# Another fixed order for layer 0's projection tiles in a two-layer hybrid trunk

## The chip, the cores and the metric

One core of a Trainium2 chip runs the whole program. The time is the device time of one execution, in microseconds (us). Of the kernel before there are three timed runs, given as their median, lowest and highest, and one profiled execution with a time of its own. Lower is better.

## The reference

The input is a residual stream of 1024 tokens by 1024 features in float32 and a conditioning vector `c`. Two layers follow, and a final RMSNorm. Each layer normalises, scales and shifts its input by values that come from `c`, runs a mixer and adds the gated result. Layer 0 is the one that the change concerns:

```python
def even_mixer(h, w_in, ...):
    p = h @ w_in
    p_a, u, v, z = jnp.split(p, [SHIFT_W, SHIFT_W + B_WIDTH, SHIFT_W + 2 * B_WIDTH], axis=-1)
    y_a = rwkv7_time_mix(p_a, ...)             # r, k, v, and two low-rank inputs
    y_b = chunked_spatial_gate(u, v, ...)      # the gated layer (gMLP)
    y = jnp.concatenate([y_a, y_b], axis=-1) * jax.nn.silu(z)
    return y @ w_out

def step(S, inp):                              # inside rwkv7_time_mix, one token after the other
    r_t, w_t, k_t, v_t, kk_t, a_t = inp
    sa = jnp.einsum('bhvk,bhk->bhv', S, -kk_t)
    S = S * w_t[:, :, None, :] + sa[..., None] * (kk_t * a_t)[:, :, None, :] + v_t[..., None] * k_t[:, :, None, :]
    y_t = jnp.einsum('bhvk,bhk->bhv', S, r_t)
    return S, y_t
```

So `h @ w_in` has columns of five kinds: r, k and v of the recurrence (8 heads of 64), u and v of the gated layer (8 groups of 64), z for the gate over both, and a low-rank part. Layer 1 is a windowed attention whose code the change leaves alone.

## The kernel before, in words

**Tiles.** A projection tile is 128 columns of `w_in`, which is two heads or two groups. It is computed in two halves of 512 tokens. One half is 24 matmuls of 128x512 into one PSUM buffer (`gproj`, line 264: eight blocks of features, each times three products of high and low parts, since float32 is split in two). The tile's weights come by two DMAs of 256 KB on SP's queue (`wfetch`, line 232) and are split by ScalarE and GpSimd (`wsplit`, line 240), one tile ahead. When a half is complete, its evacuation empties the PSUM buffer: `krv_evac` (line 316) for r, k and v, one ScalarE and one VectorE pass into one of six `krv` buffers; `z_evac`, `u_evac`, `v_evac` and `zg_evac` for the rest. There are two PSUM buffers for projections.

Tile numbers, for the pair of heads j = 0 to 3: r is j, k is 4+j, v is 8+j; u of the gated layer is 13+j, its v is 17+j; z for the recurrence's half is 21+j and z for the gated half is 25+j. Tile 12 and the first pair's k, r and v (4, 0, 8) are computed ahead of the list, in `FIRST`.

**Units.** A unit is one pair of heads over half of the tokens; there are eight, numbered 2j and 2j+1. Each goes through four steps: `front` (line 559) takes k, r and v from the `krv` buffers and makes the operands; `solve` (line 664) builds the chunk matrices (the matmuls into `A` and `pM`) and inverts them, by a loop of 30 short VectorE instructions (lines 714 and 715) between `LN` (line 702) and `ZT` (line 719); `prep` (line 776) makes the transition matrices, and its last VectorE instruction is the one on line 804; `scan` (line 807) runs the chain of states. `front` of unit n starts when its three `krv` halves are there and `solve` of unit n-1 has passed its matrices. `solve` of unit n cannot start before `front` of unit n has given it its operands.

**What sets the order.** TensorE's order is written by hand. `drive` (line 1174) is a small planner that runs when the kernel is built: it keeps a model clock, and at each turn lets the thread of highest priority that is ready issue its next piece. `scan` has priority 0, `prep` and `solve` 1, `front` 2, the gated layer's `gm_tail` 4, the conditioning rows (`do_ada`) and the output weights (`wo0_thread`) 5, and `stream` (line 989), which issues the projection tiles, 6. A `yield` with a number tells the planner how long the piece's result takes, a `yield` with a function that the thread must wait for it. So the tiles fill the spaces that the units leave on TensorE, one matmul at a time, and on the chip TensorE runs what was written in that order, and stands still where an instruction's operands are late. The other engines are ordered by the compiler's scheduler, with the units' pieces given priority.

**Rooms.** After a half's matmuls, `stream` waits for the tile's room (lines 980 to 985): for r, k and v that fewer than six `krv` buffers are held (`held`). `front` gives the three halves of a unit back one at a time: k after `f` (line 583), r after `AR` (line 621), v after `bv` (line 660), and `bv` waits until the unit two before has been posted. For z there may be two `gz` waiting, for u two `uT`, and the gated layer's v shares three buffers with the conditioning rows.

**The list.** `ORDER` (line 987) is the fixed order of the 25 tiles behind `FIRST`. Written by name it is: z0, k1, r1, v1, gv0, u0, k2, r2, z1, v2, zg0, gv1, k3, r3, z2, v3, u1, zg1, z3, gv2, u2, zg2, gv3, u3, zg3 (gv for the gated layer's v, zg for its gate).

**After the list.** `out0_thread` (line 1118) starts layer 0's output projection when the list is done, the output weights are split and all but the last unit and the last gated half are posted. `wo0_thread` can split its last nine weight tiles only when the last `scan` has been issued, because they take the recurrence's memory.

Of the kernel before, what the change touches and what calls it, by code (L numbers as in the profile page):

```python
# [93 lines left out]
def tile_kernel(ctx, tc, x, cons, par, rows, ada, ada0, ew, wup, sgw, sgb, ewo, ow, owo, out, dbg=None):  # L94
# [889 lines left out]
        evac[13 + j], room[13 + j] = u_evac(j), lambda: short[0] < 2  # L984
        evac[25 + j], room[25 + j] = zg_evac(j), lambda: True

    ORDER = (21, 5, 1, 9, 17, 13, 6, 2, 22, 10, 25, 18, 7, 3, 23, 11, 14, 26, 24, 19, 15, 27, 20, 16, 28)

    def stream():
        todo = list(ORDER)  # L990
        for i in range(4):
            if i == 1:
                raws = wfetch(ew[todo[0]])
            pt = (yield from gproj(ws[i], 1)) if i else pt1
            FIRST[i][1](1, pt)
            if i == 1:
                w = wsplit(raws)
        while todo:
            n = todo.pop(0)
            raws = wfetch(ew[todo[0]]) if todo else None  # L1000
            pt = yield from gproj(w, 0)
            yield room[n]
            evac[n](0, pt)
            if todo:
                wn = wsplit(raws)
            pt = yield from gproj(w, 1)
            yield room[n]
            evac[n](1, pt)
            if todo:
                w = wn  # L1010
        done["h1"] = new_h()
# [470 lines left out]
```

## Time and profile before

| | us |
|---|---|
| median of 3 runs | 1106.13 |
| lowest, highest | 1104.96, 1108.74 |
| the profiled execution's own time | 1109.73 |
| its span, first to last instruction | 1107.6 |
| mean granted TensorE clock over the span | 0.983 |
| TensorE busy in the span | 1040.8 |
| VectorE busy in the span | 696.3 |
| ScalarE busy in the span | 524.3 |

In the profile a line gives start and duration of an instruction in us, its engine (PE is TensorE, DVE VectorE, ACT ScalarE, POOL GpSimd, SP the queue of most DMAs), its line in the kernel, and what it writes and reads. In brackets stands how long the engine had been idle and what released it. Adjoining instructions of one kind are merged, with their number behind an x. Matmuls are pipelined: one of 128x512 is shown as about 0.39 us long, but the next one starts 0.23 us behind it.

The projection tiles of layer 0 that the list orders run from 96 us to 615 us of the span.

### The profile page before, as it was taken

The page shows a single profiled execution, that of the slowest core. Times are in us where ns is not written, and L with a number is a line of the kernel's source. Part 1 is how long each engine was busy: PE and PEld are TensorE (multiplying, and loading weights), DVE is VectorE, ACT ScalarE, POOL GpSimd, SP SyncE. Part 2 cuts the span into 40 slices and gives each one's busy share as a digit, 9 for nine tenths or more (in the row PEclk, how much of TensorE's full clock was granted, in tenths as well). Part 3 has the DMA queues.
Part 4 walks back from the last instruction along what each step waited for, and adds up shares of the span by engine and source line. Part 5 has one row for each costly group of instructions (what it writes and reads, how often), then busy time and mean ns, then how long its engine had stood idle before and what let it go on. Part 6 is the DMA issues. An engine that isn't in the chain of part 4 may idle for free. (4 is left out here: it accounts for less than half of the span.)

```text
span 1107.6 us, 20700 instructions
## 1 busy us (share of the span) xinstructions
PE 1040.8 (94%) x7887; PEld 839.4 (76%) x7888; DVE 696.3 (63%) x1668; ACT 524.3 (47%) x1247; POOL 374.7 (34%) x483
## 2 busy tenths in 40 slices
PE   6989999999988898989999899999999999999997
PEld 3667778777776676766878777778888888878886
DVE  4455958586859485595642578864565654488754
ACT  4465555454454435445332233335565654487521
POOL 2333315141335122263423100134554544467201
PEclk9989999999999899999999899999999999999999
DMA  9501121212112121123122554421110111252121
GB/s 365 224 17 39 58 77 49 68 49 77 58 61 69 46 86 58 40 79 113 60 79 74 188 183 153 156 68 39 39 39 20 39 39 39 63 176 72 63 95 58
DMA packets 55131, 93.42 MB, mean 84 GB/s; under 512 B 5748, under 2 KB 15988, under 8 KB 55032
## 3 DMA queue, kind: packets, MB, share of 16 engines
q1 hardware_dynamic: 45176, 77.36, 21.3%
q10 hardware_dynamic: 9856, 14.75, 4.2%
q8 instruction: 62, 1.02, 0.4%
q14 instruction: 37, 0.30, 0.1%
HBM read 79.49 MB, written 12.59 MB: 83 GB/s over the span
## 5 line engine op out<-in xcount | busy, mean ns | idle before, releaser
L118 PE MATMUL pproj<-lo,whi 128*128 128x512 f32 x696 | 281.2, 404 | 0.0
L118 PE MATMUL pproj<-hi,whi 128*128 128x512 f32 x696 | 279.5, 402 | 0.7 <-ACT vt L1247 0.7
L118 PE MATMUL pproj<-hi,wlo 128*128 128x512 f32 x696 | 279.7, 402 | 0.0
L246 POOL TENSOR_TENSOR wlo<-wraw,whi 128x512 fp32r<-128x512 f32 x86 | 113.8, 1343 | 167.5 <-ACT whi L245 166.5
L118 PEld LDWEIGHTS pproj<-lo,whi 128*128 128x128 f32 x696 | 131.6, 189 | 24.9 <-issue 1.5
L118 PEld LDWEIGHTS pproj<-hi,whi 128*128 128x128 f32 x696 | 131.5, 189 | 24.5 <-ACT vt L1247 1.1
L118 PEld LDWEIGHTS pproj<-hi,wlo 128*128 128x128 f32 x696 | 131.3, 189 | 24.5 <-issue 1.2
L245 ACT ACTIVATE whi<-wraw 128x512 fp32r<-128x512 f32 x102 | 58.7, 622 | 65.9 <-PE htp L122 22.1
L118 PE MATMUL op<-wo,whi 128*128 128x512 f32 x256 | 82.2, 402 | 0.0
L1283 ACT ACTIVATE Sx<-Sx,nm 128x257 f32<-128x257 f32 (+1 forms) x128 | 62.3, 489 | 27.6 <-DVE nm L1279 25.5
L1279 DVE CUSTOM_DVE_ANT_0 Sx<-pS,bias,nsink 128x256 f32<-128x256 f32 (+1 forms) x128 | 53.4, 463 | 30.1 <-PE pS L118 28.6
L1287 POOL TENSOR_SCALAR Sx<-Sx,rc 128x256 f32<-128x256 f32 (+1 forms) x128 | 60.8, 492 | 25.4 <-DVE rc L1285 22.9
L1299 DVE TENSOR_TENSOR PL<-pT,PH 128x512 fp32r<-128x512 f32 (+1 forms) x64 | 41.6, 654 | 29.7 <-ACT PH L1298 29.2
L118 PEld LDWEIGHTS op<-wo,whi 128*128 128x128 f32 x256 | 49.0, 192 | 13.0 <-issue 2.1
L925 DVE SCALAR_TENSOR_TENSOR adacc<-araw,cond,adacc 128x512 f32<-128x512 f32 x56 | 44.0, 786 | 18.5 <-DMA araw<-ada 18.4
L118 PE MATMUL op<-hi,yh 128*128 128x512 f32 (+1 forms) x136 | 51.8, 381 | 0.4 <-ACT yh L1397 0.4
L118 PE MATMUL op<-hi,yl 128*128 128x512 f32 (+1 forms) x136 | 51.7, 380 | 0.4 <-DVE yl L1398 0.4
L118 PE MATMUL op<-wo,wlo 128*128 128x512 f32 x128 | 51.7, 404 | 0.0
L118 PE MATMUL op<-lo,yh 128*128 128x512 f32 (+1 forms) x136 | 51.5, 379 | 0.0
L213 POOL TENSOR_TENSOR st<-st,nhalf 128x1 f32<-128x1 f32 x16 | 9.6, 602 | 102.6 <-DVE st L212 91.0
L714 DVE TENSOR_TENSOR pr<-Lf,LT 128x2 f32<-128x2 f32 (+14 forms) x120 | 42.5, 354 | 2.7
L1298 ACT ACTIVATE PH<-pT 128x512 fp32r<-128x512 f32 (+1 forms) x64 | 35.7, 563 | 17.5 <-PE pT L1293 16.2
(317 smaller groups left out, 2166.5 us busy)
## 6 DMA issues: line engine op xcount, KB each, us to landing
araw<-ada SPq DMA_DIRECT2D x64, 256.0 KB, 2.8
wraw<-ew SPq DMA_DIRECT2D x50, 256.0 KB, 3.0
wraw<-ow SPq DMA_DIRECT2D x36, 256.0 KB, 3.0
adaraw<-ada SPq DMA_DIRECT2D x16, 512.0 KB, 9.0
x<-x SPq DMA_DIRECT2D x8, 512.0 KB, 8.7
woraw<-ewo SPq DMA_DIRECT2D x16, 256.0 KB, 2.9
xr<-x ACTq DMA_DIRECT2D x16, 256.0 KB, 3.5
wraw<-y0d SPq DMA_DIRECT2D x16, 256.0 KB, 3.1
```

The source lines that it names most:

```text
L118: last[0] = nc.tensor.matmul(out, lhsT=lhsT, rhs=rhs, **kw).ins
L213: G.tensor_tensor(out=st[:, 3:4], in0=st[:, 2:3], in1=nhalf[:, 0:1], op=ALU.pow)
L245: a = S.activation(hi[:, gs, :], raws[g], AF.Copy)
L246: b = E.tensor_tensor(out=lo[:, gs, :], in0=raws[g], in1=hi[:, gs, :].bitcast(F32), op=ALU.subtract)
L714: V.tensor_tensor(out=pr[:, 0:nc_, 0:i + 1], in0=Lf[:, i:i + 1, 0:i + 1].to_broadcast([P, nc_, i + 1]), in1=LTt[:, 0:nc_, 0:i + 1], op=ALU ...
L925: op = V.scalar_tensor_tensor(out=acc, in0=raw, scalar=cond[:, k:k + 1], in1=acc, op0=ALU.mult, op1=ALU.add)
L1279: V.tensor_tensor_reduce(out=Sx[:, e, off:2 * P], in0=pS3[:, e, 0:nk], in1=bias[e][:, off:], scale=1.0, scalar=nsink[:, hd:hd + 1], op0=AL ...
L1283: S.activation(pr[:, e, off:2 * P + 1], Sx[:, e, off:2 * P + 1], AF.Exp, bias=nm[:, e:e + 1], scale=-1.0, accum_out=sm[:, e:e + 1])
L1287: G.tensor_scalar(out=pr[:, e, off:2 * P], in0=pr[:, e, off:2 * P], scalar1=rc[:, e:e + 1], scalar2=0.5, op0=ALU.mult, op1=ALU.mult)
L1298: S.activation(PH[:, ks, :], pT2[:, ks, :], AF.Copy)
L1299: V.tensor_tensor(out=PL[:, ks, :], in0=pT2[:, ks, :], in1=PH[:, ks, :].bitcast(F32), op=ALU.subtract)
```

## The change

One line is changed, the list:

```diff
-    ORDER = (21, 5, 1, 9, 17, 13, 6, 2, 22, 10, 25, 18, 7, 3, 23, 11, 14, 26, 24, 19, 15, 27, 20, 16, 28)
+    ORDER = (21, 5, 1, 9, 17, 6, 2, 10, 22, 13, 25, 7, 3, 11, 23, 18, 14, 26, 24, 19, 15, 27, 20, 16, 28)
```

By name, the part that differs:

```
before  ... gv0, u0, k2, r2, z1, v2, zg0, gv1, k3, r3, z2, v3, u1, zg1 ...
after   ... gv0, k2, r2, v2, z1, u0, zg0, k3, r3, v3, z2, gv1, u1, zg1 ...
```

In the list k2 and r2 come one tile earlier, v2 two, u0 four later; k3 and r3 come one tile earlier, v3 two, gv1 four later. The tiles before gv0, zg0 in the middle, and everything from u1 on keep their places in the list. What is computed is the same. Because `drive` writes TensorE's order out anew from the list, where each matmul of the tiles falls between the units' pieces can change from there to the end of layer 0.

## Prediction

> **What bounds the kernel now.** I read the page first, then busy time by stretches, then the timeline of TensorE, VectorE and ScalarE around each unit of the recurrence. Columns of a stretch: the stretch and its length; busy us of PE, PEld, DVE, ACT and POOL (instructions); granted clock, DMA share, GB/s.
>
> ```profile
> PE 1040.8 (94%) x7887; PEld 839.4 (76%) x7888; DVE 696.3 (63%) x1668; ACT 524.3 (47%) x1247; POOL 374.7 (34%) x483
> ```
>
> ```profile
> 100.00:300.00 200.00, 187.86 (x1994) 149.03 (x1993) 143.96 (x348) 100.63 (x230) 58.15 (x49) 1.00 0.20 62
> 300.00:500.00 200.00, 177.55 (x1820) 139.76 (x1818) 137.42 (x309) 92.67 (x210) 66.80 (x51) 0.97 0.20 62
> ```
>
> TensorE is the bound, and in this stage it is filled by the tiles that the list orders. Its work is the same before and after, so only its idle time and its slow clock can be won. In 100 to 300 us it idles 12.1 us, in 300 to 500 us 22.4 us, with the clock down to 0.97. The difference, 10.3 us of idle time, and 0.03 x 200 = 6.0 us of clock are the most that a better order could win there.
>
> What the change aims at is the recurrence. VectorE's line 804 ends a unit's `prep`, its line 690 is the first product of the next unit's matrices. Units 1 to 2, 3 to 4 and 5 to 6:
>
> ```profile
> 209.84 0.69 DVE L804 TENSOR_TENSOR PA<-pn,dC 128x512 f32<-128x512 f32 x1
> 212.73 0.42 DVE L690 TENSOR_TENSOR BR<-A,rcon 128x256 f32<-128x256 f32 x1 [1.55 <-PE pM L118]
> 319.76 0.68 DVE L804 TENSOR_TENSOR PA<-pn,dC 128x512 f32<-128x512 f32 x1
> 326.26 0.42 DVE L690 TENSOR_TENSOR BR<-A,rcon 128x256 f32<-128x256 f32 x1 [1.25 <-PE pM L118]
> 445.71 0.69 DVE L804 TENSOR_TENSOR PA<-pn,dC 128x512 f32<-128x512 f32 x1
> 463.08 0.42 DVE L690 TENSOR_TENSOR BR<-A,rcon 128x256 f32<-128x256 f32 x1 [1.69 <-PE pM L118]
> ```
>
> The step takes 2.9 us, then 6.5, then 17.4. The excess, 3.6 and 14.5 us, are units 4 and 6 waiting for their `front`, and that waited for v2 and v3:
>
> ```profile
> 289.05 0.67 ACT L301 ACTIVATE krv<-pproj,der 128x512 f32<-128x512 f32 x1
> 394.31 1.07 DVE L702 STREAM_TRANSPOSE LN<-Dg 128x512 f32<-128x512 f32 x1
> 424.87 0.69 ACT L301 ACTIVATE krv<-pproj,der 128x512 f32<-128x512 f32 x1
> 430.80 0.68 DVE L583 TENSOR_TENSOR f<-krv,f 128x512 f32<-128x512 f32 x1
> ```
>
> `front` of unit 6 was free to start when unit 5 had its matrices (`LN`, 394.3 us), but v3's first half was evacuated at 424.9 us and `f` followed at 430.8.
>
> **When the moved tiles arrive.** No row shows the new order, so I take the stream's places as they are and put the new tiles into them. v2's first half takes the place of r2's, v3's first half that of r3's:
>
> ```profile
> 249.28 0.69 ACT L301 ACTIVATE krv<-pproj,der 128x512 f32<-128x512 f32 x1
> 273.91 1.04 DVE L702 STREAM_TRANSPOSE LN<-Dg 128x512 f32<-128x512 f32 x1
> 395.74 0.69 ACT L301 ACTIVATE krv<-pproj,der 128x512 f32<-128x512 f32 x1
> 594.06 0.28 DVE L821 SCALAR_TENSOR_TENSOR PA<-chain,dC,PA 128x64 f32<-128x64 f32 x1 [1.56 <-PE chain L118]
> ```
>
> So v2 comes near 249 instead of 289 us, v3 near 396 instead of 425. The first is 25 us ahead of unit 3's `LN` (273.9), the second 1.4 us behind unit 5's. Both waits should go: the last scan ends some 3.6 + 14.5 = 18 us sooner than at 594.3 us (the last of these rows).
>
> ```profile
> 440.00:460.00 20.00, 19.38 (x151) 15.41 (x151) 8.93 (x20) 8.54 (x17) 6.05 (x4) 1.00 0.12 41
> ```
>
> That is not 18 us of time. In the long wait, at 440 to 460 us, TensorE idled 0.6 us: it had tiles to run. With the wait gone those tiles are run elsewhere: more are left over behind the last scan, each half at its bare length, as two neighbouring halves show:
>
> ```profile
> 543.39 0.60 ACT L955 ACTIVATE uT<-pproj 128x512 f32<-128x512 f32 x1 [0.74 <-PE pproj L118]
> 548.86 0.60 ACT L955 ACTIVATE uT<-pproj 128x512 f32<-128x512 f32 x1 [4.87 <-PE pproj L118]
> ```
>
> A half costs 5.5 us wherever it stands; 24 matmuls moved are 24 matmuls. The same holds for what goes with a tile: its two DMAs on SP (256 KB, 3.0 us to landing), two splits on ScalarE and two on GpSimd are issued once per tile, a tile of two halves ahead, so at least 11 us of TensorE cover 3.0 us of fetch. I cost them at nothing; without that cover a tile would cost up to 3.0 us.
>
> ```profile
> wraw<-ew SPq DMA_DIRECT2D x50, 256.0 KB, 3.0
> ```
>
> **The sum: which stalls go.**
>
> ```profile
> 420.00:440.00 20.00, 16.09 (x251) 12.14 (x251) 11.30 (x16) 12.62 (x28) 6.81 (x5) 0.91 0.23 67
> 432.00:436.00 4.00, 4.00 (x43) 3.48 (x35) 2.82 (x4) 1.71 (x4) 1.21 (x2) 0.57 0.21 65
> ```
>
> ```profile
> 431.76 0.69 PE L118 MATMUL pM<-Zq,M 32*32 32x32 f32 x32 [1.80 <-ACT M L766]
> 310.29 1.94 PE L118 MATMUL uw<-PA,Z 128*128 128x128 f32 x15 [1.41 <-ACT Z L773]
> ```
>
> First, unit 6's late `front` runs into the end of unit 5's `solve`: the 1.80 us stall waits for a small copy on ScalarE behind that `front`'s activations. Stretch 420 to 440 idles 3.9 us where the rate of 100 to 300 us gives 20 x 12.1/200 = 1.2. Gain 2.7, at most 3.9 and at least nil, if the planner puts another stall there. Second, behind that stall the clock is halved for a piece: 0.09 x 20 = 1.8 us lost in the stretch. Gain 1.8. Third, unit 4's late `front` does the same at the end of unit 3's `solve`: gain 1.4 (bounds 0 and 1.4, since a weight split stood in ScalarE's way there too). Fourth, a cost: the two `front`s now run in a place that was empty; 440 to 460 idled 0.6 us instead of 1.2, and by the same rate I charge 0.6 for it. Fifth, the end of the stage:
>
> ```profile
> 614.06 1.19 DVE L1104 TENSOR_TENSOR wo<-woraw,wo 128x512 fp32r<-128x512 f32 x1
> 615.17 0.16 DVE L886 TENSOR_SCALAR gst<-gst 128x8 f32<-128x8 f32 x1
> 615.05 0.60 ACT L851 ACTIVATE ggz<-pproj 128x512 f32<-128x512 f32 x1 [1.09 <-PE pproj L118]
> 617.99 1.98 PE L118 MATMUL mix<-sgwt,vn 128*64 128x128 f32 x16 [3.26 <-DVE vn L890]
> ```
>
> TensorE stands 3.26 us for the last gated half, whose statistics (615.17) queue on VectorE behind a 1.19 us split of output weights. These splits wait for the last scan, so with the scan 18 us earlier they are over by then. Gain 1.2 of the 3.26; the rest, the gated half's own chain behind zg3, stays late.
>
> The tiles that move back, u0 and gv1, cost nothing in this sum: zg0 and zg1, which use what they leave, keep their places, and u0 and gv1 are still ahead of them, with u1 between gv1 and zg1 (two halves, 11 us). If that is too short for gv1's statistics, TensorE stands as at the last `mix`, up to 3.26 us.
>
> Sum: 2.7 + 1.8 + 1.4 - 0.6 + 1.2 = 6.5 us. The profiled execution would go from 1109.73 to 1103.2. It lies 3.6 us above the median of 1106.13; the same gain from the median gives 1099.6. Layer 1 keeps its code and its order, and I put no change there.
>
> A rule to weigh: the rows show the clock at 0.57 behind a stall of 1.80 us, but TensorE back at 1.00 for the whole of 440 to 460. The Trainium skill, "TensorE: Matmul & The Clock Gate", section "HAM oscillation — how this bites in real kernels", states that idle gaps above about 3.4 us are to be avoided. By that alone a 1.80 us stall halves nothing and the second term would be nil, a sum of 4.7; the trace disagrees, and I keep 1.8. The same page, "What's actually happening", has the activity window run freely, by which a like stall may or may not cost a piece.
>
> **The rivals.** *No change worth measuring.* The planner writes a new interleaving, and the stalls move. For it: 300 to 500 us has other stalls that have nothing to do with v2 and v3. The largest is unit 4's `ZT`, 3 us behind a loop that shares VectorE with zg0's evacuation and the gated layer's tail, and a slow clock after it:
>
> ```profile
> 361.57 0.65 PE L118 MATMUL pM<-ZT,Dg 16*32 16x32 f32 x32 [2.99 <-DVE ZT L719]
> 364.00:368.00 4.00, 4.00 (x75) 3.13 (x74) 1.31 (x4) 1.48 (x4) 0.00 (x0) 0.56 0.15 50
> ```
>
> Stretch 364 to 368 loses 0.44 x 4 = 1.8 us, with the stall 4.8. One new collision of that kind leaves 6.5 - 4.8 = 1.7 us of gain: 1104.4.
>
> *Slower.* VectorE becomes the late one in the loops of units 3 and 5. These had no `front` beside them; unit 2's loop had one. `LN` and `ZT` of unit 2, then `ZT` of units 3 and 5 (their `LN` stand above) with the matmul that takes it:
>
> ```profile
> 219.16 1.04 DVE L702 STREAM_TRANSPOSE LN<-Dg 128x512 f32<-128x512 f32 x1 [0.93 <-ACT Dg L696]
> 238.42 0.40 DVE L719 TENSOR_TENSOR ZT<-Tm,rcon 128x256 f32<-128x256 f32 x1
> 288.83 0.42 DVE L719 TENSOR_TENSOR ZT<-Tm,rcon 128x256 f32<-128x256 f32 x1
> 298.45 0.75 PE L118 MATMUL pM<-ZT,Dg 16*32 16x32 f32 x64
> 412.37 0.42 DVE L719 TENSOR_TENSOR ZT<-Tm,rcon 128x256 f32<-128x256 f32 x1
> 420.01 0.75 PE L118 MATMUL pM<-ZT,Dg 16*32 16x32 f32 x64
> ```
>
> With a `front` the stretch from `LN` to `ZT` takes 19.3 us in unit 2, without one 14.9 in unit 3: a `front` costs about 4.4. TensorE takes unit 3's `ZT` 9.2 us after it is ready and unit 5's 7.2, so 4.8 and 2.8 us would be left. It decides when the loop of unit 5 grows by over 7.2 us and that of unit 3 by over 9.2. If both do, two collisions of unit 4's kind cost 9.6, and with the clock halved twice as long, as the rows cannot exclude, 13.2: 3 to 7 us slower, 1109 to 1113. Against it: both have room left.
>
> *The change doesn't do what it says.* v2's second half needs a free `krv` buffer, given back by unit 3's `bv`:
>
> ```profile
> 253.86 0.69 DVE L660 TENSOR_TENSOR bv<-bon,krv 128x512 f32<-128x512 f32 x1
> 258.85 0.69 ACT L301 ACTIVATE krv<-pproj,der 128x512 f32<-128x512 f32 x1 [0.40 <-PE pproj L118]
> ```
>
> The buffer is free at 253.9 and the half's place ends at 258.9, 5.0 us of room. If the stream stops there, everything behind it on TensorE's list loses one half of filler, 5.5 us, and the gain shrinks to 1.0: 1105.1.
>
> **How the numbers follow.** About 0.3%, 3.3 us, is what a measurement of this kernel can tell from no change. The forecast has 0.50, no change 0.25, VectorE late 0.20, the stopped stream 0.05. Of the forecast 0.03 fall within 3.3 us; the no-change case gives 0.03 to faster and 0.02 to slower, VectorE late 0.03 to same, the stopped stream 0.02 to faster and 0.03 to slower. Faster 0.52, same 0.26, slower 0.22. The low end takes the whole excess idle time and the end term plus half of the clock's 6.0: 10.3 + 1.2 + 3.0 = 14.5, 1091.6. The high end is near that of VectorE late, 1112. The forecast's own range is 1091.6 to 1102.8, the upper end being a gain of 3.3 with the second and third term at nil.
>
> **What would show it.** Right: line 804 to 690 within 4 us at units 4 and 6; `f` of unit 6 near 400 us; the last scan near 576; 300 to 500 us idling under 18 us with a clock of 0.98 or more; the stall before the last `mix` near 2 us; zg3's last evacuation near 609 instead of 615.05. Wrong: a `ZT` stall at units 3 or 5, a stall of 2 us or more at a place that had none, or the scan early and zg3 not.

## The result, and the profile after

| | before | after |
|---|---|---|
| median, us | 1106.47 | 1098.41 |
| lowest, highest | 1104.96, 1108.74 (4 runs) | 1097.57, 1100.28 (4 runs) |
| the profiled execution: span, own time | 1107.6, 1109.73 | 1096.3, 1098.15 |
| mean granted clock in the profiled execution | 0.983 | 0.992 |

The change is faster: the ratio is 0.9928, with a 95% interval of 0.9906 to 0.9949, or 8.1 us. The prediction was 1099.6 us. The profiled executions differ by more, 11.3 us of span, because the one of before had a slower clock than its kernel usually has: over the 59 timed executions of the kernel before that this study has, the mean span is 1105.5 us and the clock 0.988, which is 1105.5 x 0.012 = 13.3 us lost to it; over the four of after 1096.8 us and 10.2 us lost. By this estimate, which counts every half-clock microsecond as half lost and sets executions on several chips side by side, some 3 of a mean gain of 8.7 us are clock and 5.5 are time in which TensorE works instead of standing.

The two stretches of the prediction, for after (columns as there):

```profile
100.00:300.00 200.00, 186.32 (x1994) 147.98 (x1994) 147.15 (x353) 104.86 (x239) 62.55 (x51) 1.00 0.20 62
300.00:500.00 200.00, 182.93 (x2088) 144.66 (x2088) 142.87 (x325) 96.15 (x222) 62.30 (x50) 0.97 0.21 65
```

From 300 to 500 us TensorE idles 17.1 us instead of 22.4, from 100 to 300 it idles 13.7 instead of 12.1. The clock of the stretch is the same to two decimals.

The handovers to units 4 and 6 in after, VectorE's timeline; then v2's and v3's first halves, unit 6's `f` and the last scan:

```profile
319.55 0.69 DVE L804 TENSOR_TENSOR PA<-pn,dC 128x512 f32<-128x512 f32 x1
323.12 0.42 DVE L690 TENSOR_TENSOR BR<-A,rcon 128x256 f32<-128x256 f32 x1 [2.23 <-PE pM L118]
440.06 0.69 DVE L804 TENSOR_TENSOR PA<-pn,dC 128x512 f32<-128x512 f32 x1
443.21 0.42 DVE L690 TENSOR_TENSOR BR<-A,rcon 128x256 f32<-128x256 f32 x1 [1.20 <-PE pM L118]
```

```profile
247.85 0.69 ACT L301 ACTIVATE krv<-pproj,der 128x512 f32<-128x512 f32 x1
391.20 0.69 ACT L301 ACTIVATE krv<-pproj,der 128x512 f32<-128x512 f32 x1
396.54 0.68 DVE L583 TENSOR_TENSOR f<-krv,f 128x512 f32<-128x512 f32 x1
570.99 0.28 DVE L821 SCALAR_TENSOR_TENSOR PA<-chain,dC,PA 128x64 f32<-128x64 f32 x1 [1.56 <-PE chain L118]
```

Both waits are gone: 3.6 us where there were 6.5, 3.2 where there were 17.4. The last scan is 23.1 us earlier. Of these 23 us, 2.1 were there before the first moved tile, as is shown next; of the other 21, 6 reach the last projection.

Where the 11.3 us of the two profiled executions lie is seen at two marks, the evacuation of the last gated half and the first score matmul of layer 1. The evacuation in after (that of before, at 615.05 us, stands in the prediction), then the score matmul in before and in after:

```profile
606.88 0.60 ACT L851 ACTIVATE ggz<-pproj 128x512 f32<-128x512 f32 x1 [2.40 <-PE pproj L118]
757.91 0.22 PE L118 MATMUL pS<-KH,Q 128*128 128x128 f32 x1
746.60 0.22 PE L118 MATMUL pS<-KH,Q 128*128 128x128 f32 x1
```

The first mark comes 615.05 - 606.88 = 8.2 us sooner, the second 11.3: the end of layer 0 gives another 3.1, and layer 1 gives nothing. Of the 8.2, 2.1 stand ahead of the first tile that changed place (gv0's last half is evacuated at 196.3 us in before and 194.2 in after), and there TensorE's order is the same; it is clock:

```profile
60.00:80.00 20.00, 17.43 (x72) 11.82 (x71) 10.99 (x14) 13.25 (x26) 5.76 (x6) 0.82 0.08 23
60.00:80.00 20.00, 16.63 (x73) 11.26 (x72) 12.28 (x16) 15.04 (x29) 7.62 (x9) 0.91 0.08 24
```

The first row is of before, the second of after: 0.09 x 20 = 1.8 us. So the 11.3 us are 2.1 of clock that have nothing to do with the change, 6.0 between gv0 and the last projection, and 3.1 behind it. In the 6.0, TensorE's idle time falls from 31.4 to 26.2 us and the clock loses 5 us instead of 7.

**The stalls that went.** The 1.80 us at unit 5's matrices, the 1.12 us at its `uw` behind it, the 1.41 us at unit 3's `uw` and 1.60 us at unit 6's `ZT` (501 us) are not there any more. Nor is a stall that the prediction did not see, at the first gated half behind zg1. Before, then after:

```profile
482.02 1.09 PE L118 MATMUL mix<-sgwt,vn 128*64 128x128 f32 x16 [3.26 <-DVE bst L897]
481.60 1.09 PE L118 MATMUL mix<-sgwt,vn 128*64 128x128 f32 x16
```

Behind it the clock of before is 0.79 from 482 to 490 us, 1.7 us lost; in after it is 1.00 there.

At the end of the stage, in after:

```profile
593.50 0.70 DVE L1104 TENSOR_TENSOR wo<-woraw,wo 128x512 fp32r<-128x512 f32 x1 [1.85 <-ACT wo L1103]
606.62 0.62 PE L118 MATMUL op<-wo,whi 128*128 128x512 f32 x2
608.34 1.09 PE L118 MATMUL mix<-sgwt,vn 128*64 128x128 f32 x16
```

The last split of output weights ends at 594.2 instead of 615.2 us, and TensorE has begun the output projection (`op`) before the last `mix`; it does not stand there at all. In before a slow piece follows that stall, 0.43 x 8 = 3.4 us lost; in after the clock is 1.00 from 604 to 624 us:

```profile
616.00:624.00 8.00, 6.01 (x27) 4.89 (x28) 2.80 (x4) 1.09 (x2) 2.35 (x2) 0.57 0.77 252
```

Stall and clock are 6.7 us. Only 3.1 of them are gained, mainly because in after the time from the last matmuls of the output projection to layer 1's first score is 3.0 us longer (38.7 instead of 35.8).

**The stalls that came.** The largest is at unit 5's `ZT`. VectorE's `LN` and `ZT` of unit 5 and TensorE's taking of it, the clock behind it, and the loop's stretch in before (first) and after (second):

```profile
389.73 1.06 DVE L702 STREAM_TRANSPOSE LN<-Dg 128x512 f32<-128x512 f32 x1 [0.56 <-ACT Dg L696]
417.62 0.41 DVE L719 TENSOR_TENSOR ZT<-Tm,rcon 128x256 f32<-128x256 f32 x1
418.09 0.75 PE L118 MATMUL pM<-ZT,Dg 16*32 16x32 f32 x64 [2.83 <-DVE ZT L719]
420.00:424.00 4.00, 3.71 (x73) 2.45 (x72) 2.89 (x5) 2.51 (x7) 0.00 (x0) 0.61 0.14 53
```

```profile
394.00:413.00 19.00, 18.15 (x163) 15.08 (x162) 18.10 (x52) 6.07 (x13) 6.55 (x7) 1.00 0.35 100
390.00:418.00 28.00, 23.64 (x194) 18.64 (x193) 26.91 (x65) 14.89 (x28) 14.78 (x13) 1.00 0.22 67
```

From `LN` to `ZT` it is 27.9 us instead of 18.1, and VectorE is busy in 26.91 of 28.00 us: unit 6's `front` now runs beside unit 5's loop, VectorE takes 9.8 us longer to give `ZT`, and TensorE stands 2.83 us for it and then runs slowly for a piece. Smaller stalls came with it: 1.45 us at unit 4's `bkt` (294 us), 1.24 at unit 3's `pn` (318) and 1.55 at unit 5's `kb` (346).

### The profile page after: what moved, and what is told of

Read it like the earlier page. It is cut to its first block, busy times and chain, and to the rows that moved or that the text cites. A ratio compares the mean times of both kernels' runs of the same rounds, so it can differ in the third digit from the quotient of the medians.

```text
span 1096.3 us, 20701 instructions
## 1 busy us (share of the span) xinstructions
PE 1034.2 (94%) x7888; PEld 833.1 (76%) x7888; DVE 697.3 (64%) x1668; ACT 524.5 (48%) x1247; POOL 372.9 (34%) x483
## 4 chain that ended last, share of the span: by engine, by line
PE 60%; DVE 22%; ACT 5%; DMA 4%; issue 3%; POOL 1%; ACTq 0%; POOLq 0%; DVEq 0%; SPq 0%
PE pproj L118 34%; PE op L118 8%; PE po L118 2%; PE pS L118 2%; PE pM L118 2%; DVE pr L714 2%; PE pT L1293 2%; DVE adacc L925 2%; DMA araw<-ada 2%; DVE hf L228 2%; PE uw L118 1%; ACT Dg L696 1%; DVE LT L715 1%; PE pn L118 1%; PE A L118 1%
## 5 line engine op out<-in xcount | busy, mean ns | idle before, releaser
L118 PEld LDWEIGHTS op<-wo,whi 128*128 128x128 f32 x256 | 48.1, 188 | 12.5 <-issue 1.0
L714 DVE TENSOR_TENSOR pr<-Lf,LT 128x2 f32<-128x2 f32 (+14 forms) x120 | 44.2, 368 | 2.6
```

The source lines that it names most:

```text
L118: last[0] = nc.tensor.matmul(out, lhsT=lhsT, rhs=rhs, **kw).ins
L714: V.tensor_tensor(out=pr[:, 0:nc_, 0:i + 1], in0=Lf[:, i:i + 1, 0:i + 1].to_broadcast([P, nc_, i + 1]), in1=LTt[:, 0:nc_, 0:i + 1], op=ALU ...
```

## The experiments

The first theory, A, was the prediction's: the gain comes from unit 6's `front` being on time, and unit 4's and the gated tiles' new places are worth little. Its rivals stand in the expectations. When it fell, theory C took its place: VectorE's load alone decides. That fell too, and the last one was formed, of **two kinds of stall**: a late `front` is the cause of one kind, a full or waiting VectorE of the other; the change trades stalls of the first kind for some of the second, and what it is worth depends on what VectorE has to do. Each ratio is to runs of the kernel before on the same chip (medians of 1107.2 to 1107.9 us).

### Each half of the change alone

Only the second pair moved, and only the third:

```diff
-    ORDER = (21, 5, 1, 9, 17, 13, 6, 2, 22, 10, 25, 18, 7, 3, 23, 11, 14, 26, 24, 19, 15, 27, 20, 16, 28)
+    ORDER = (21, 5, 1, 9, 17, 6, 2, 10, 22, 13, 25, 18, 7, 3, 23, 11, 14, 26, 24, 19, 15, 27, 20, 16, 28)  # pair 2
+    ORDER = (21, 5, 1, 9, 17, 13, 6, 2, 22, 10, 25, 7, 3, 11, 23, 18, 14, 26, 24, 19, 15, 27, 20, 16, 28)  # pair 3
```

Expected of pair 2 alone:

> Only the first half of the change: k2, r2 and v2 in a row with u0 behind z1; pair 3 as before (gv1, k3, r3, z2, v3). Theory A (the gain comes from the recurrence no longer waiting for v2 and v3: units 5 to 7 get ahead of the gated tiles they used to collide with, and the last weight splits are over before the list ends): unit 4's wait goes, unit 6 still waits some 14 us for v3, the last scan is 3 to 5 us earlier than before, the stall at the last mix (3.3 us) and its slow clock stay: 1103 to 1107 us. Theory B (any other order moves the stalls about, and this one fell well): the time is not tied to unit 6's wait, anything from 1097 to 1110 us, and in particular a time near 1098 with unit 6 still waiting would speak for B.

Measured: 1112.08 us, ratio 1.0047 (1.0032 to 1.0063), slower. Unit 6's wait is still there (line 804 at 438.87, line 690 at 456.25 us),

```profile
475.62 1.09 PE L118 MATMUL mix<-sgwt,vn 128*64 128x128 f32 x16 [2.51 <-DVE bst L897]
```

and with it the `mix` stall behind zg1 (2.51 us, the row) and the one at the end (3.54 us). The time is outside of both theories' ranges. Expected of pair 3 alone:

> Only the second half of the change: k3, r3 and v3 in a row with gv1 behind z2; pair 2 as before. Theory A: unit 4 waits 3.6 us as before, unit 6 does not, the last scan is 15 to 18 us earlier than before, the stall at the last mix and its slow clock are gone: 1097 to 1101 us, most of the change's gain. Theory B: not tied to it, 1097 to 1110 us.

Measured: 1106.57 us, ratio 1.0000 (0.9989 to 1.0012), no change. Here Theory A fell: unit 6's wait is gone, the last scan is at 575.45 us, neither `mix` stands, and nothing is gained. Two stalls ate it, 3.28 us at unit 5's `ZT` and one of 3.39 us further on, TensorE's and then VectorE's timeline, and the clock behind it:

```profile
481.47 0.90 PE L122 MATMUL yt<-con,sqy 128*128 128x128 f32 x3 [3.39 <-ACT PA L652]
477.42 1.55 DVE L925 SCALAR_TENSOR_TENSOR adacc<-araw,cond,adacc 128x512 f32<-128x512 f32 x1 [1.23 <-DMA araw<-ada]
479.49 0.28 DVE L744 TENSOR_TENSOR Zq<-Zq,pM 128x128 f32<-128x128 f32 x1
480.00:494.00 14.00, 12.53 (x109) 9.63 (x110) 7.80 (x11) 5.44 (x15) 3.45 (x3) 0.51 0.37 117
```

To be read from the second row: VectorE stood 1.23 us for a conditioning row that was still on its way, then took 1.55 us to sum it, and behind that in its line, after one evacuation, stood unit 6's inverse (`Zq`), behind this ScalarE's copies of `Z` and of `PA`, and behind those TensorE. After it TensorE ran at 0.51 of its clock for 14 us: 6.9 us lost.

The halves do not add up: +4.9 us and nothing, where both together give -8.1.

### The conditioning rows left out

In these kernels seven of the eight terms of the sums for layer 1's scale and layer 0's gate are left out, so VectorE has 28 instructions of 0.74 us less, and 28 transfers fewer to wait for. It was put on after, on before, and on pair 3 alone:

```diff
             for k in range(KC):
+                if k and (layer, part) in ((1, 1), (0, 2)):
+                    continue
```

> The changed kernel without the conditioning rows' additions on VectorE for the scale of layer 1 and the gate of layer 0: seven of eight terms of each sum are left out (28 instructions of 0.74 us), their loads stay. If VectorE's load makes ZT late in the loops of units 4 and 5: the stalls at ZT (2.6 and 2.8 us in the changed kernel) fall under 1 us and their slow clock pieces go (5.1 us lost in all): 1089 to 1094 us. If ZT is late for another reason (GpSimd's instructions beside VectorE's, or the order on TensorE): the stalls stay, 1096 to 1099 us.

> The kernel before with the same additions of the conditioning rows left out as in e4 (28 instructions of 0.74 us on VectorE). Theory A fell with e2. Theory C: TensorE's stops come from VectorE, where a unit's loop of short instructions meets other VectorE work; the order matters only by what it lets meet. Then, with that load lighter, the two orders lie close: 1089 to 1093 us beside e4's 1088.8. Rival A2 (the waits of units 4 and 6 for v2 and v3 cost time by themselves, whatever VectorE does): the distance of 8 us stays, 1095 to 1099 us.

> The order with only the third pair moved, leaving out seven of the eight terms of the conditioning-row sums for layer 1's scale and layer 0's gate. Theory of two kinds of stall: unit 6's wait is gone in this order, and without the rows the stalls set by VectorE are gone too, so it comes near the changed kernel without rows (1088.8) and far from the kernel before without rows (1104.8): 1089 to 1095, the third pair doing most of it. Rival (the halves simply add, the third pair being worth nothing): 1103 to 1106.

| ratio to before | with the rows | without |
|---|---|---|
| order of before | 1 | 0.9972 (0.9961 to 0.9983) |
| pair 3 alone | 1.0000 (0.9989 to 1.0012) | 0.9890 (0.9875 to 0.9905) |
| after | 0.9928 (0.9906 to 0.9949) | 0.9833 (0.9816 to 0.9850) |

The medians without the rows are 1104.77, 1095.03 and 1088.79 us. In all three orders TensorE's matmuls come in the traces in the same sequence with the rows and without (in after one of them has moved by a few places, at 501 us), so what differs is VectorE's list. After came out just under the expected 1089 us, before slower than either theory had said (1089 to 1093, 1095 to 1099). Theory C fell here, since with the rows gone the two orders lie further apart and not closer. Without the rows the change is worth 1.4% (0.9972 to 0.9833, some 15 us) instead of 0.7%, and pair 3 alone, worth nothing with the rows, is worth 0.8%. In the order of before the rows cost about 3 us, in that of after about 10: with unit 6's late `front` TensorE stands anyway, and what VectorE does meanwhile matters little. The stretch from 300 to 500 us, in the order of before and of after, both without the rows:

```profile
300.00:500.00 200.00, 178.68 (x1895) 141.56 (x1894) 128.03 (x295) 94.81 (x215) 64.07 (x52) 0.97 0.21 65
300.00:500.00 200.00, 189.31 (x2201) 150.17 (x2202) 135.40 (x324) 101.87 (x237) 64.63 (x53) 1.00 0.23 75
```

In the first TensorE still idles 21.3 us, in the second 10.7 at full clock. The stalls of before that stayed without the rows are those at unit 5's matrices (1.80 us) and at the two `mix` (2.84 and 3.28): these belong to unit 6's late `front`. The one at unit 3's `uw` stands wherever unit 4's `front` is late, and is longer without the rows (3.14 us instead of 1.41, and 3.07 in pair 3 alone). Those that went are at `ZT`: these belong to VectorE. This is what the theory of two kinds of stall expects. It was put on record for pair 3 alone, which came out at the upper edge of its range.

### The rows moved in time, or to other engines

First, rows held back while the loops of units 4 and 5 run (`looping` is set in `solve` ahead of the loop and cleared behind it):

```diff
+                if (layer, part) in ((1, 1), (0, 2)):
+                    yield lambda: not looping[0]
```

> The changed kernel, all work kept, but the additions of these rows are held back while the loops of units 4 and 5 run; they are made up later, where VectorE is less busy. Theory C: the stalls at these units' ZT (2.6 and 2.8 us) and the slow clock behind them (5.1 us lost in all) mostly go: 1092 to 1096 us. Rival (the rows only shift the meeting elsewhere): 1097 to 1101 us.

Measured: 1100.79 us, ratio 0.9938 (0.9921 to 0.9954). Both `ZT` stalls went, but the time is the rival's. In the profiled execution, the slowest of six (1103.93 us), the gain went into 2.74 us at unit 4's `bkt` and into the stall that pair 3 alone has, at its place and by the same chain: TensorE, then VectorE's row (the sum stands three lines lower in this kernel), then the clock behind:

```profile
477.20 1.11 PE L122 MATMUL yt<-con,sqy 128*128 128x128 f32 x4 [3.52 <-ACT PA L652]
473.40 0.91 DVE L928 SCALAR_TENSOR_TENSOR adacc<-araw,cond,adacc 128x512 f32<-128x512 f32 x1 [1.38 <-DMA araw<-ada]
476.00:490.00 14.00, 12.79 (x111) 9.89 (x112) 6.29 (x11) 5.43 (x15) 1.53 (x2) 0.51 0.37 119
```

Then rows summed later, so that they should have landed: one number of the planner's, put on pair 3 alone and on after:

```diff
-"do_ada1": 4.5
+"do_ada1": 6.5
```

> The order with only the third pair moved, and the planner told that a conditioning row takes 6.5 us to arrive instead of 4.5 (one number). With the plain order of this kind VectorE stood 1.23 us for a row that had not arrived and then summed it, all ahead of the inverse of unit 6 (line 744), and TensorE stood 3.39 us for the line 652 copies behind it, with a half clock of 13.7 us after. VectorE theory: the rows stand later on VectorE's list, their waits in the stage fall from about 13 us to under 6, the 3.39 us stall and the piece behind it go, 1096 to 1101 us. Rival (the stall at unit 6 comes from the order itself, its front being 18 us sooner): the stall stays over 2.5 us, 1105 to 1108.

> The changed kernel with the same one number. VectorE theory: its waits for rows fall from 14 us to under 6, the stall at unit 5's ZT from 2.83 to under 1.5, 1093 to 1097 us, a ratio of 0.988 to 0.991. Rival (waits for rows cost nothing in this order, only the sums themselves do): as the changed kernel, 1097 to 1100.

Measured: 1115.55 us, ratio 1.0070 (1.0058 to 1.0083), and 1110.14 us, ratio 1.0021 (1.0010 to 1.0032). Both times are outside of what either theory expected. What was to be mended was mended. VectorE's waits for rows between 78 and 615 us (total us, times, the longest), in pair 3 alone and with the number changed, then in after and with it:

```profile
DVE adacc L925 <- DMA araw<-ada: 12.8, 7, 3.1
DVE adacc L925 <- DMA araw<-ada: 2.4, 2, 1.5
DVE adacc L925 <- DMA araw<-ada: 14.2, 9, 3.2
DVE adacc L925 <- DMA araw<-ada: 3.7, 4, 1.4
```

The 3.39 us stall of the one is gone, and unit 5's `ZT` stall of the other is down from 2.83 to 1.41 us. But the same number also moved the matmuls by which TensorE totals a sum (`adac`), and in both kernels TensorE stands ahead of them 5.36 us. TensorE and the clock behind, with the later rows in after:

```profile
185.46 1.05 PE L118 MATMUL gvn<-con,vT 128*128 128x128 f32 x8
194.95 1.20 PE L118 MATMUL adac<-ones,adacc 128*128 128x1 f32 x5 [5.36 <-DVE vn L890]
192.00:203.00 11.00, 8.05 (x88) 6.50 (x89) 2.23 (x5) 2.89 (x9) 1.98 (x2) 0.53 0.01 1
```

It is not the rows that TensorE stands for: the sum's last row was added by 179.9 us. The totals go to a PSUM buffer of which there is one (`pg`, line 141), the gated layer's `gvn` had taken it just before, and `vn`, which by the profile ends the stall, is what reads `gvn`. In after the totals come first, at 169.1 us, and `gvn` at 182.4. The stall and 0.47 x 11 = 5.2 us of clock are 10.5 us, as much as lies between this kernel and after (a ratio of 1.0021 against 0.9928, 10 us). So the experiment brought in a stall of another kind, and does not tell what mending the waits is worth.

Last, seven of eight steps of every sum taken off VectorE, with nothing left out:

```diff
-                    op = V.scalar_tensor_tensor(out=acc, in0=raw, scalar=cond[:, k:k + 1], in1=acc, op0=ALU.mult, op1=ALU.add)
+                    paced(S.activation(raw, raw, AF.Copy, scale=cond[:, k:k + 1]))
+                    op = G.tensor_tensor(out=acc, in0=raw, in1=acc, op=ALU.add)
```

> The changed kernel with seven of the eight steps of each conditioning-row sum taken from VectorE: ScalarE multiplies the row by its scalar, GpSimd adds it (its additions of 128x512 take 1.4 us by the rows of the changed kernel, some 56 of them). Nothing is left out. VectorE theory: the stalls at unit 4's and 5's ZT (2.56 and 2.83 us) and the half clock behind them go as they did when the rows were left out (1088.8), no new stall of over 2 us: 1089 to 1095. Rival one (it is not VectorE's time but the rows' late transfers that block whatever engine stands in line for them): GpSimd or ScalarE stands for the rows, the operands and weight splits behind it are late, 1098 to 1108. Rival two (GpSimd's additions lengthen VectorE's instructions beside them): VectorE's 128x512 steps in the stage lengthen, 1095 to 1100.

Measured: 1118.29 us, ratio 1.0089 (1.0072 to 1.0105), the slowest of all, worse than its first rival allowed, though TensorE's matmuls come in the same sequence as in after (with the one exception above). The `ZT` stalls went, and the waits moved to the engines that now stand for the rows (ScalarE, then GpSimd behind it):

```profile
ACT araw L925 <- DMA araw<-ada: 26.7, 21, 3.5
POOL adacc L926 <- ACT araw L925: 66.9, 24, 7.5
```

ScalarE waits 21 times for a row with its evacuations of PSUM behind it in line, which is the first rival's mechanism. The second rival's part is small: up to 605 us the 120 steps of line 714 take 47.1 us instead of 44.2. Here an engine that was half idle was no place for an instruction that waits.

### The order of other parts, and the end

Two more orders. In the first, of the order of before only v2 is exchanged with z1 and v3 with z2, so that each v comes one place later than in after and u0 and gv1 stay early. In the second u0 and gv1 go back as in after, and each v stays behind its z:

```diff
-    ORDER = (21, 5, 1, 9, 17, 13, 6, 2, 22, 10, 25, 18, 7, 3, 23, 11, 14, 26, 24, 19, 15, 27, 20, 16, 28)
+    ORDER = (21, 5, 1, 9, 17, 13, 6, 2, 10, 22, 25, 18, 7, 3, 11, 23, 14, 26, 24, 19, 15, 27, 20, 16, 28)  # v before z
+    ORDER = (21, 5, 1, 9, 17, 6, 2, 22, 10, 13, 25, 7, 3, 23, 11, 18, 14, 26, 24, 19, 15, 27, 20, 16, 28)  # gated tiles back
```

> The kernel before with v2 ahead of z1 and v3 ahead of z2, u0 and gv1 left where they were. Unit 4's wait goes, unit 6's wait of 14 us shrinks to 3 us or less. A2: most of the change's gain, 1098 to 1102 us. Theory C: what meets in the loops decides, and neither wait tells it: the stage is then no nearer to the changed kernel's than to the kernel before, 1101 to 1112 us.

Measured: 1104.89 us, ratio 0.9975 (0.9963 to 0.9987), a gain of 2.8 us. Unit 4's wait goes (3.6 us), but unit 6 is still 4 us late (line 804 at 440.73, line 690 at 447.70 us), which was not expected.

> The change without its swaps: u0 and gv1 moved back as in the change, v2 left behind z1 and v3 behind z2. Unit 4's wait goes, unit 6's wait of 14 us shrinks to 3 us or less. A2: 1098 to 1102 us, like the change. Theory C: decided by what meets in the loops, 1097 to 1112 us; a time away from e5's with the same waits gone speaks for C.

Measured: 1108.63 us, ratio 1.0012 (1.0000 to 1.0024). Here unit 6 is some 3.5 us late (line 804 at 447.04, line 690 at 453.47 us), and the `mix` behind zg1 stands 3.02 us again; its clock is 0.74 from 424 to 444 us. Both miss A2's range. But in neither is unit 6's wait gone, so they do not tell what an order without the waits is worth. Of the five orders tried beside that of before, after gains 8 us, v before z a third of that, and the other three nothing or less.

Finally after with the last output weights' splits held back until the last unit is posted, so that they come late again:

```diff
-                yield lambda: hopped[0] == 8
+                yield lambda: hopped[0] == 8 and posted[0] == 8
```

> The changed kernel, but the last nine output weight tiles may be split only when the last unit is posted, not when its scan is issued, so that they fall into the last 17 us of the list again. Theory A: up to 585 us all is as in the changed kernel; then the first matmul of the output projection comes 2 to 5 us later behind the last projection, with a piece of slow clock worth 1 to 3 us: 1101 to 1106 us. Rival (the end of the stage got shorter only because the planner wrote the last mix behind the first output matmuls, whatever the splits do): no difference, 1097 to 1100 us.

Measured: 1098.97 us, ratio 0.9931 (0.9903 to 0.9958), the same as after. The last `mix` stands again, about half as long as in before, and layer 1 begins as early, since what follows the output projection is shorter by as much:

```profile
606.26 1.09 PE L118 MATMUL mix<-sgwt,vn 128*64 128x128 f32 x16 [1.76 <-DVE vn L890]
```

So the gain at the end of layer 0 does not hang on the splits' being early. What this kernel shares with after there is the clock, 1.00 from 600 to 620 us, while before loses 3.4 us behind its stall.

No version here beats after. Leaving out part of the sums gives 1088.8 us, so some 10 us lie in the rows; none of three ways to move them got at it. A second buffer for the rows, by which they could be fetched one ahead, was not tried.

## Why the prediction was right, and where not

**Right: the waits.** v2 came at 247.9 us (predicted near 249), v3 at 391.2 (396), `f` of unit 6 at 396.5 (near 400), the last scan at 571.0 (near 576), and both handovers are within 4 us. The places of the stream carried over to the moved tiles within 5 us. With the 2.1 us by which the whole profile of after is early taken off, v2 came at 250.0, v3 at 393.3, the last scan at 573.1 and zg3's last evacuation at 609.0, which is the 609 that was predicted. That 18 us of scan would not be 18 us of time was right too.

**Right total, wrong parts.** The sum was 6.5 us of gain and 8.1 were measured. Term by term:

- *First and second term (2.7 and 1.8 us, unit 6's late `front` against the end of unit 5's `solve`).* The stalls went as said; the order of before without rows, where unit 6's wait stays, keeps them (1.80 and 1.12 us). But in their place came unit 5's `ZT` stall of 2.83 us and 0.39 x 4 = 1.6 us of clock behind it: 4.4 us, nearly the whole 4.5 of the two terms.
- *Third term (1.4 us at unit 3's `uw`).* That stall went; 1.24 us at unit 3's `pn` and 1.55 at `kb`, in unit 4's loop, came.
- *Fourth term (0.6 us for two `front`s in a new place).* This is the step that failed. It charged a rate of idle time, where the cost is VectorE's: the `front` adds about 9 us to a loop. Without the rows, before and after, unit 3's loop takes 12.6 and 21.6 us and unit 5's 15.5 and 24.4.
- *Fifth term (1.2 of the 3.26 us at the end).* Mis-sized: the end of layer 0 gave 3.1 us. The prediction left the gated half's own chain late, a stall of some 2 us; in after TensorE runs the output projection's first matmuls in that time and does not stand. It also put the term down to the weight splits, and with these late the time is the same, with a stall of 1.76 us. And it put the clock behind that stall at nothing, where the profile of before lost 3.4 us.
- *Not in the sum:* 3.26 us at the `mix` behind zg1, and 1.7 us of clock behind it, which went. The prediction took unit 4's 2.99 us for the largest stall of the stretch and overlooked this one; it named the `mix` only as a place where a stall might come. It stands in four kernels (before, with the rows and without, pair 2 alone, gated tiles back), in each of which unit 6 took over 6 us from line 804 to 690, and in none in which it took under 4; in one order, v before z, it is missing at 7.0 us, so the late `front` goes with it and is not all of its cause. gv1's place does not decide it: with gv1 moved back it stands in one order (gated tiles back) and not in two (pair 3 alone, after).

**The slower rival was half right.** It named VectorE late in the loops of units 3 and 5, and said that both had room: 9.2 and 7.2 us, for a `front` of 4.4. The price was too low: the 4.4 came from comparing unit 2's loop with unit 3's, and unit 3's had other work in it, rows that take 2.3 of its 14.9 us among it. From `LN` to `ZT` unit 3 went from 14.9 to 24.9 us and unit 5 from 18.1 to 27.9: 10.0 and 9.8. Unit 5's is past its 7.2, and TensorE stood 2.8 us, which is what 9.8 - 7.2 = 2.6 gives. Unit 3's `ZT` was given at 297.1 us, past its 9.2 too, and taken at once, since TensorE had just stood 1.45 us at `bkt`; with the late splits, where TensorE's order is the same up to 606 us, it stood 1.64 us here:

```profile
272.21 1.04 DVE L702 STREAM_TRANSPOSE LN<-Dg 128x512 f32<-128x512 f32 x1 [0.34 <-ACT Dg L696]
297.10 0.42 DVE L719 TENSOR_TENSOR ZT<-Tm,rcon 128x256 f32<-128x256 f32 x1
297.58 0.75 PE L118 MATMUL pM<-ZT,Dg 16*32 16x32 f32 x64
```

Had the price been known, the place at unit 5 would have counted for sure and that at unit 3 been on the edge: 6.5 - 4.4 = 2.1 us of gain by the prediction's own terms, no change worth measuring. What kept the result at 8 us are gains that no term held: the `mix` behind zg1, the rest of the end, and the clock. One of the signs that the prediction itself had named for being wrong, a `ZT` stall at unit 5, came. The forecast's number was right in part by offsetting errors, and that part is luck.

**The clock.** The prediction kept 1.8 us for a half clock behind a stall of 1.80 us. That piece went, and so did the one behind the `mix` at 482 us; one of the same kind came. The stretch of 300 to 500 us has 0.97 as before, not the 0.98 that was to be seen. Over all timed executions the change gains some 3 us of clock by the estimate above, so the clock did its part, but not only at the place named.

**What stays open.** A row that has not landed stands ahead of unit 6's inverse in after too, and VectorE waits 1.30 us for it. But there the inverse has to wait for TensorE's `pM` behind it anyway:

```profile
475.73 0.75 DVE L925 SCALAR_TENSOR_TENSOR adacc<-araw,cond,adacc 128x512 f32<-128x512 f32 x1 [1.30 <-DMA araw<-ada]
477.91 0.29 DVE L744 TENSOR_TENSOR Zq<-Zq,pM 128x128 f32<-128x128 f32 x1 [1.42 <-PE pM L118]
```

So the row costs nothing in after, and in pair 3 alone it costs a stall of 3.39 us. It follows from what the planner had written on TensorE around that place; no rule was found by which it could have been foretold. An order that looks nearly as good as after's can come out 8 us slower, as pair 3 alone does.

## What to carry to other kernels

When a late operand is brought forward, its producer's work goes where there was none before: add up that engine's busy time in the new place, from rows, and compare it with the room that the waiting engine has there. Do not price it by the difference of two places that differ in other work too. And an instruction that waits for a transfer holds up everything behind it on its engine; whether that costs depends on what the others wait for there. Moving it to a less busy engine need not shorten the wait: 14.2 us of it on VectorE became 26.7 on ScalarE, and 66.9 on GpSimd behind that.

## What the runs showed of the hardware

**VectorE beside GpSimd.** In unit 5's loop, two of VectorE's instructions with two operands in SBUF stretch while GpSimd works, and one with an operand in PSUM does not. VectorE and then GpSimd in after:

```profile
410.19 1.37 DVE L714 TENSOR_TENSOR pr<-Lf,LT 128x120 f32<-128x120 f32 x1
411.48 1.79 DVE L925 SCALAR_TENSOR_TENSOR adacc<-araw,cond,adacc 128x512 f32<-128x512 f32 x1
413.19 0.68 DVE L557 TENSOR_TENSOR sqy<-py,niy 128x512 f32<-128x512 f32 x1
409.64 1.67 POOL L611 TENSOR_TENSOR qb<-qb,f 128x512 f32<-128x512 f32 x1
411.27 3.15 POOL L246 TENSOR_TENSOR wlo<-wraw,whi 128x512 fp32r<-128x512 f32 x2
```

The step of 1.37 us ends 0.25 us behind GpSimd's `qb` (411.31), and the row's sum, 0.74 us elsewhere, takes 1.79 beside the next split; line 557, whose `py` lies in PSUM, takes its usual 0.68 beside the second. This agrees with the Trainium skill, "SBUF — State Buffer", section "Who interferes with whom": the two engines share a pair of ports under an exclusive lock, and a VectorE instruction with two SBUF inputs contends with a GpSimd instruction that reads SBUF. Two operands are not the whole of it: line 620, with one, took 1.27 us beside a split in after (290.4 us) and 0.16 at 470.3. GpSimd's part in the loop grew from 6.55 to 14.78 us with the `front`, so some of the 10 us by which the loop grew may be this; how much was not measured by itself.

**The clock behind a stall.** Stalls of 1.80 us (before), 2.83 us (after), 3.39 and 3.52 us (pair 3 alone, rows held back) were followed by a clock of 0.57 for 4 us, 0.61 for 4 us, and 0.51 for 14 us each. In the long ones TensorE was busy for 12.5 and 12.8 of the 14 us and the clock did not come back within them. One such piece, 6.9 us, is nearly the size of the whole change, so two orders with the same idle time can lie 7 us apart. From 100 us to the end of the list the slow pieces of all these profiles are at half clock and last 3.4 us or two, three or four times that.

The same stall does not always cost one. At unit 4's `ZT` TensorE stood 2.56 us in after and 2.59 in the kernel with late splits, whose order is the same up to 606 us. The clock there, in after and then with the late splits:

```profile
358.00:368.00 10.00, 8.68 (x174) 6.72 (x176) 4.89 (x9) 6.60 (x16) 2.57 (x2) 0.66 0.18 56
358.00:368.00 10.00, 8.43 (x219) 6.50 (x219) 5.35 (x11) 7.79 (x19) 2.68 (x2) 1.00 0.24 80
```

That is 3.4 us between two executions of the same order, so a slow piece seen in one profile is one sample.
